# A decoder block with latent attention and gated linear attention: where its gate tiles are made, how v is spilled, and two smaller moves

## The chip, the cores and the metric

The kernel runs on one core of one Trainium2 chip. The metric is the device time of one execution in microseconds, from three runs. The core has TensorE (matmul; the profile calls it PE, and PEld its weight loads), VectorE (DVE), ScalarE (ACT), GpSimd (POOL) and SyncE (SP, which here only issues transfers).

## The reference, cut to what matters

With x of 1024 positions and 1024 channels, one layer computes

```
h = rmsnorm(x, g_in);  proj = h @ w_in
c_q, c_kv, k_r, z_mla, q_g, k_g, v_g, a_lr, z_gla, gate_mla, gate_gla = split(proj)
q = rmsnorm(c_q) @ w_uq  (8 heads, 64 + 32 columns, the 32 with rotary);  k_nope, v_mla = rmsnorm(c_kv) @ w_ukv
o_mla = softmax(q k^T / sqrt(96), causal) v_mla;  y_mla = (o_mla * silu(z_mla)) @ w_proj_mla
o_gla = chunked gated linear attention(q_g, k_g, v_g, log_a)  (4 heads, k 128, v 256)
y_gla = (rmsnorm(o_gla) * silu(z_gla)) @ w_proj_gla
out = rmsnorm(x + (sigmoid(gate_mla) * y_mla + sigmoid(gate_gla) * y_gla) @ w_out, g_final)
```

All in float32. The kernel keeps that precision by splitting each operand into a rounded part and a rest ("hi" and "lo", tiles named `...h` and `...l`) and adding three matmuls, hi x hi, hi x lo and lo x hi.

## The kernel before

The 1024 positions are two halves of 512. The program has these stages, in this order:

1. Projections of both halves together (`blocks`, matmuls at L390, tiles `prod`). VectorE and ScalarE add products (L732), split operands (`split`, L193 cast on ScalarE, L194 subtraction, on VectorE) and turn the results into what later stages read; these go to HBM: `gqd` (q, k and k transposed of the linear attention, split), `gvd` (its v, transposed, split), `latd`, `szd`, `xnd` (the normalised x of half 1).
2. Gated linear attention, 8 groups (2 halves x 4 heads). `fetch` loads a group's `qk` and `vv`; `scores_and_states`, `outputs`, `normalise` and `turn` work one group behind another. `tables` makes the rotary tables for each half beside it.
3. Attention of half 0 (8 heads), output of half 0 (`yg`, `ym` and `wo` units), then the same for half 1.

Beside stages 2 and 3 runs a stream of units (`Stream`): each has weights that are loaded (L161, tile `wraw`), split (L170 and L171, tiles `whi` and `wlo`; the subtraction goes to VectorE or GpSimd as the unit says) and used in steps of 6 matmuls (L184, tile `pj`). The units of a half stand in one list: gate tiles (`g0` to `g15`, 24 matmuls of 512 columns, tanh at L806 into `zr`, then stored to `gtd` from ScalarE's queue at L807), `uqr` (rotary part of the queries), `uv`, `hi0` to `hi3` (queries and keys of two heads each), `yg`, `ym`, `wo`. `GATES[h]` says how many gate tiles stand before `uqr` and after each `hi`: (10, 2, 2, 1, 1) for half 0 and (1, 4, 5, 4, 2) for half 1. The stream stops at a unit that is fenced, until the main program opens it. The main program calls `st.step(n)` between its own parts, so the gates are the work that TensorE does while a head waits for other engines. A list scheduler then sets the order of each engine.

One head of the attention: `row_max` computes scores against the keys a first time (L1240), adds the mask to the diagonal block (L1245), takes the maximum (L1247), and puts its negative into two extra query rows (L1255, L1256, L1261, L1264); this is done one head ahead. `scores` then computes the scores (L1284 to L1287), adds the mask (L1289), takes the exponential (L1293), splits it (L1296, L1297), sums it on GpSimd (L1299), and `values` multiplies by v (L1305, L1306). `linear_inputs` loads the linear attention's result during heads 5 and 6 in eight pieces of 256 KB through two `zr` buffers and splits each. The query tile `qt` holds 64 columns from `hi`, the 32 rotary ones (copied by ScalarE at L869 from `qr`) and the two extra rows.

In the output of half 0, `prologue` loads `xnd` in eight pieces and splits it into `xh` and `xl`, the operands of half 1's gates; those can start only afterwards (fence `1g0`).

## Time and profile before

| | us |
|---|---|
| median of three runs (1125.98 to 1134.52) | 1129.0 |
| the profiled execution | 1128.2 |
| its span, first to last instruction | 1126.4 |
| mean granted clock of TensorE | 0.962 |

The profile is of that one execution. A row by stage gives, for each engine, the time that it was busy in the stretch and the number of instructions; PEclk is the mean granted clock as a share of 2.4 GHz, and the last columns are the busy share of the 16 DMA engines and what they moved. A row of a group of instructions gives their line, engine, operation, out<-in with shapes and count, then busy time and mean ns of one, then the idle time of the engine just before them with what ended it. In a timeline a row is start, length, engine, line, operation, and in brackets the idle time before it and what ended that. "ACTq" is a transfer issued by ScalarE's queue, "SPq" one issued by SyncE's.

### The profile page before, as it was taken

How to read it: one execution, taken by the hardware profiler on the slowest of the kernel's cores; microseconds unless marked ns; L12 is line 12 of the kernel's file. 1: busy time of each engine (PE TensorE's matmuls, PEld its weight loads, DVE VectorE, ACT ScalarE, POOL GpSimd, SP SyncE). 2: the span in 40 equal slices, each digit the busy share in tenths (PEclk: the TensorE clock that was granted, in tenths of full speed). 3: DMA queues.
4: the chain of work that ended last, by engine and by line, in shares of the span. 5: the costliest groups of instructions: out<-in, count | busy, mean ns of one | idle time of the engine just before them, and what ended most of it. 6: DMA issues, size and time to landing. Idle time of an engine off the chain costs nothing.

```text
span 1126.4 us, 14090 instructions
## 1 busy us (share of the span) xinstructions
PE 1048.0 (93%) x4817; PEld 845.8 (75%) x4817; DVE 762.3 (68%) x1305; ACT 584.6 (52%) x1074; POOL 228.5 (20%) x173
## 2 busy tenths in 40 slices
PE   8999998999999878997898889999899999899997
PEld 4878887888888667875676667888678786678775
DVE  6885678788886535856766766476656768677463
ACT  5754374656574316765566553254565557434232
POOL 0000000000000000021433222123455555233320
PEclk9999999999999989999989779999999999899899
DMA  7452648555735598986624237744733233324432
GB/s 283 169 202 81 232 145 299 203 189 186 251 123 187 177 399 294 325 325 211 220 68 122 85 93 273 248 143 152 213 105 107 85 108 122 110 84 132 158 113 94
DMA packets 83992, 200.34 MB, mean 178 GB/s; under 512 B 8704, under 2 KB 21376, under 8 KB 83792
## 3 DMA queue, kind: packets, MB, share of 16 engines
q1 hardware_dynamic: 75856, 182.66, 48.1%
q10 hardware_dynamic: 8064, 16.78, 4.0%
q8 instruction: 38, 0.62, 0.2%
q14 instruction: 34, 0.28, 0.1%
HBM read 135.57 MB, written 63.83 MB: 177 GB/s over the span
## 4 chain that ended last, share of the span: by engine, by line
PE 37%; DVE 7%; ACT 3%; DMA 3%; issue 2%; POOL 1%; POOLq 0%; DVEq 0%; ACTq 0%; SPq 0%
PE pj L184 23%; PE y L924 2%; PE y L922 2%; PE y L923 2%; PE sc L1284 2%; DVE pl L1297 1%; DVE mx L1247 1%; PE sc L1286 1%; PE sc L1287 1%; PE ov L1306 1%; PE sc L1240 1%; PE ov L1305 1%; DMA zr<-gtd 1%; DMA wraw<-in_dram 1%; DMA kb<-krsp 1%
## 5 line engine op out<-in xcount | busy, mean ns | idle before, releaser
L184 PE MATMUL pj<-xl,whi 128*128 128x512 f32 x384 | 139.2, 411 | 2.1 <-ACT xl L193 2.1
L170 ACT CAST whi<-wraw 128x1024 fp32r<-128x1024 f32 (+2 forms) x84 | 85.0, 1012 | 94.4 <-PE pj L184 65.8
L184 PE MATMUL pj<-xh,whi 128*128 128x512 f32 x256 | 106.1, 414 | 17.1 <-ACT whi L170 14.7
L1299 POOL TENSOR_TENSOR acc<-acc,p 128x512 f32<-128x512 f32 (+3 forms) x80 | 85.4, 1068 | 151.3 <-ACT p L1293 137.5
L171 POOL TENSOR_TENSOR wlo<-wraw,whi 128x1024 fp32r<-128x1024 f32 (+2 forms) x33 | 73.6, 2230 | 94.7 <-ACT whi L170 54.3
L184 PEld LDWEIGHTS pj<-xl,whi 128*128 128x128 f32 x384 | 76.9, 201 | 18.7 <-ACT xl L193 2.5
L1297 DVE TENSOR_TENSOR pl<-p,ph 128x512 fp32r<-128x512 f32 (+3 forms) x80 | 69.7, 878 | 27.1 <-ACT ph L1296 27.0
L171 DVE TENSOR_TENSOR wlo<-wraw,whi 128x1024 fp32r<-128x1024 f32 x51 | 66.3, 1299 | 29.5 <-ACT whi L170 24.4
L732 DVE TENSOR_TENSOR ring<-prod,ring 128x512 f32<-128x512 f32 x85 | 58.4, 688 | 40.8 <-PE prod L390 38.0
L246 POOL TENSOR_TENSOR orn<-ms,mhalf 128x4 f32<-128x4 f32 x8 | 8.4, 1049 | 343.5 <-DMA zr<-in_dram 284.1
L184 PE MATMUL pj<-lat,whi 128*128 128x512 f32 x264 | 76.5, 429 | 0.1
L184 PEld LDWEIGHTS pj<-xh,whi 128*128 128x128 f32 x256 | 51.1, 200 | 28.6 <-ACT whi L170 15.5
L1293 ACT ACTIVATE p<-sc 128x512 f32<-128x512 f32 (+3 forms) x80 | 37.3, 469 | 65.7 <-DVE sc L1289 42.0
L184 PE MATMUL pj<-xh,wlo 128*128 128x512 f32 x256 | 70.3, 397 | 0.0
L193 ACT CAST w7h<-sw 128x512 fp32r<-128x512 f32 x68 | 41.8, 619 | 51.4 <-PE prod L390 45.9
L1247 DVE TENSOR_REDUCE mx<-sc 128x1 f32<-128x512 f32 (+2 forms) x96 | 51.7, 552 | 23.3 <-PE sc L1240 22.3
L184 PEld LDWEIGHTS pj<-lat,whi 128*128 128x128 f32 x264 | 53.5, 208 | 12.4 <-issue 0.6
L184 PEld LDWEIGHTS pj<-xh,wlo 128*128 128x128 f32 x256 | 48.1, 191 | 9.8
L390 PE MATMUL prod<-xl,w7h 128*128 128x512 f32 x136 | 54.1, 399 | 1.4 <-DVE xl L194 1.4
L390 PE MATMUL prod<-xh,w7h 128*128 128x512 f32 x136 | 54.7, 403 | 0.3 <-ACT w7h L193 0.2
L193 ACT CAST w7h<-raw 128x512 fp32r<-128x512 f32 x51 | 31.3, 619 | 38.2 <-PE prod L390 32.8
L924 PE MATMUL y<-whi,zl 128*128 128x512 f32 x128 | 50.4, 396 | 0.7 <-DVE zl L194 0.7
(300 smaller groups left out, 2706.7 us busy)
## 6 DMA issues: line engine op xcount, KB each, us to landing
wraw<-in_dram SPq DMA_DIRECT2D x74, 512.0 KB, 4.0
raw<-in_dram SPq DMA_DIRECT2D x32, 512.0 KB, 4.0
qk<-gqd SPq DMA_DIRECT2D x24, 512.0 KB, 6.5
gqd<-hl SPq DMA_DIRECT2D x16, 512.0 KB, 4.7
gvd<-hl SPq DMA_DIRECT2D x16, 512.0 KB, 3.6
vv<-gvd SPq DMA_DIRECT2D x16, 512.0 KB, 5.9
gtd<-zr ACTq DMA_DIRECT2D x32, 256.0 KB, 2.1
zr<-gtd SPq DMA_DIRECT2D x32, 256.0 KB, 2.9
```

Of the source, the lines that this page charges most:

```text
L170: nc.scalar.copy(out=hi[:, 0:n], in_=raw[:, 0:n])
L171: getattr(nc, lo_engine).tensor_tensor(out=lo[:, 0:n], in0=raw[:, 0:n], in1=R(hi[:, 0:n]), op=ALU.subtract)
L184: nc.tensor.matmul(out=ps, lhsT=a, rhs=b, start=(i == 0), stop=(i == 3 * n - 1))
L193: cast = nc.scalar.copy(out=hi, in_=src)
L390: mm = nc.tensor.matmul(out=ps, lhsT=a, rhs=b, start=(j == 0 and i in (1, 6, 7, 5)), stop=(j == 11), skip_group_check=True)
L732: nc.vector.tensor_tensor(out=t, in0=ps, in1=y, op=ALU.add)
L922: nc.tensor.matmul(out=c.ops[t], lhsT=a[0], rhs=b[0], start=(k == 0), stop=False)
L924: nc.tensor.matmul(out=c.ops[t], lhsT=a[1], rhs=b[0], start=False, stop=(k == 7))
L1247: nc.vector.reduce_max(mx[:, t, b:b + 1], ps[:, 0:n], axis=mybir.AxisListType.X)
L1293: nc.scalar.activation(p[:, 0:n], ps[:, 0:n], AF.Exp, scale=SCALE)
L1297: nc.vector.tensor_tensor(out=pl[:, 0:n], in0=p[:, 0:n], in1=R(ph[:, 0:n]), op=ALU.subtract)
L1299: nc.gpsimd.tensor_tensor(out=s.acc[:, q0:TH], in0=s.acc[:, q0:TH], in1=p[:, 0:n], op=ALU.add)
```

## The change

- Gates. `GATES` becomes (12, 4, 0, 0, 0) for half 0 and (0, 4, 3, 2, 1) for half 1, and the first six gate tiles of half 1 move into half 0's list: three before `hi2`, two before `hi3`, one before `yg0`. For these the rest of the weights (`wlo`) is made on VectorE. `gtd` gets a slot for each half.
- So that half 1's `xh` and `xl` exist by then, `prologue` runs during head 1 of half 0, through the two `zr` buffers; `m2` and `uh`, `ul` of half 0, which used the memory of `xh` and `xl`, get their own.
- Fewer steps of the stream in the heads of half 1 (5 in each of heads 0 to 5 and 12 in heads 6 and 7, where it was 11 in each); 6 in each head of half 0 instead of 4 and then 8.
- v is spilled in float32, unsplit: one store of 256 KB from ScalarE's queue for each piece instead of one of 512 KB from SyncE's, and `fetch` loads one 512 KB tile `vr` and splits it on chip instead of loading two.
- The second group's `fetch` stands behind three weight loads instead of beside the first. `gla` and `gla2` change places in memory, and `wgs`, `rst` and `gst` move.
- Mask and row maximum become one VectorE instruction for the block that has the diagonal (with a second one that reads the accumulator), and the maximum over both blocks of half 1 is chained through it.
- The rotary query rows `qt[64:96]` are moved by a transfer from SyncE's queue instead of a ScalarE copy.

```diff
-GATES = ((10, 2, 2, 1, 1), (1, 4, 5, 4, 2))
+GATES = ((12, 4, 0, 0, 0), (0, 4, 3, 2, 1))
+BORROW = (3, 2, 1)
...
-            rv = mk(pl, [P, TH], F32, "xs", bufs=bufs)
+            rv = mk(up, [P, TH], F32, "zr", bufs=2)
             nc.sync.dma_start(out=rv, in_=xnd[kt])
...
-                    o = hl()
-                    split(o[:, 0, :], o[:, 1, :], tp)
-                    move(gvd[h, g, vt], o)
+                    o = ring()
+                    nc.scalar.copy(out=o, in_=tp)
+                    nc.scalar.dma_start(out=gvd[h, g][:, vt, :], in_=o)
...
-                    nc.scalar.copy(out=qt[64:96], in_=R(c.qr[rr, hd // 4]))
+                    move(qt[64:96], c.qr[rr, hd // 4])
...
+    us0, us1 = units_of(0), units_of(1)
+    ahead = us1[:sum(BORROW)]
+    del us1[:sum(BORROW)]
+    for n, name in zip(BORROW, ("0hi2", "0hi3", "0yg0")):
+        k = next(i for i, u in enumerate(us0) if u.name == name)
+        us0[k:k] = ahead[:n]
+        del ahead[:n]
...
+            vr = mk(gp2, [P, 2, 4, P], F32, "vr")
+            nc.sync.dma_start(out=vr, in_=gvd[h, g].rearrange("p a (c f) -> p a c f", c=4))
             vv = mk(gp2, [P, 2, 2, 4, P], F32R, "vv")
-            for vt in range(2):
-                move(vv[:, vt].rearrange("p a c f -> p a (c f)"), gvd[h, g, vt])
+            split(vv[:, 0], vv[:, 1], vr)
...
         fetch(*cores[0])
-        fetch(*cores[1])
         for _ in range(4):
-            st.step(2)
+            st.step(3)
+        with tc.issue_after(loads[-3].ins):
+            fetch(*cores[1])
...
-                            nc.vector.tensor_tensor(out=ps[:, n - P:n], in0=ps[:, n - P:n], in1=msk[:, 1, :],
-                                                    op=ALU.add)
-                        nc.vector.reduce_max(mx[:, t, b:b + 1], ps[:, 0:n], axis=mybir.AxisListType.X)
+                            nc.vector.tensor_tensor_reduce(out=ps[:, 0:n], in0=ps[:, 0:n], in1=mrow[:, TH - n:TH], scale=1.0,
+                                                           scalar=NEG if b == 0 else mx[:, t, 0:1], op0=ALU.add,
+                                                           op1=ALU.max, accum_out=mx[:, t, b:b + 1])
+                        else:
+                            nc.vector.reduce_max(mx[:, t, b:b + 1], ps[:, 0:n], axis=mybir.AxisListType.X)
...
+                if hd == 1 and h == 0:
+                    lin = prologue()
...
-                    tick((1 if hd < 5 else 2) if h == 0 else (1, 2, 1, 1, 2, 1, 2, 1)[kt])
+                    tick((2, 1, 2, 1)[kt] if h == 0 else ((1, 0, 1, 1, 0, 1, 1, 0) if hd < 6 else (2, 1) * 4)[kt])
+                    if hd == 1 and h == 0:
+                        next(lin, None)
+                        if kt == 3:
+                            for _ in lin:
+                                pass
+                            st.fences.discard("1g0")
```

SyncE's queue where the linear attention begins, before: the weights of the third gate (the last row but two) stand behind both groups' `qk` (3822 to 3826 the first group's, 3831 to 3835 the second's) and the first `vv`.

```order
L161 DMA wraw<-in_dram 128x1024 x2
L991 DMA msk<-in_dram 128x384
L203 DMA qk_3822<-gqd 128x1024
L203 DMA qk_3824<-gqd 128x1024
L203 DMA szd<-ring 128x512
L203 DMA qk_3826<-gqd 128x1024
L203 DMA vv<-gvd 128x1024 x2
L203 DMA qk_3831<-gqd 128x1024
L203 DMA qk_3833<-gqd 128x1024
L203 DMA qk_3835<-gqd 128x1024
L161 DMA wraw<-in_dram 128x1024
L203 DMA vv<-gvd 128x1024 x2
```

The same place after, from the first group's v on (`vr`); 3914 and 3916 are the second group's `qk`, and L164 is the weight load.

```order
L1081 DMA vr<-gvd 128x1024
L1154 DMA sz<-szd 128x512 x2
L206 DMA lat_5284<-latd 128x1024
L164 DMA wraw<-in_dram 128x1024
L206 DMA lat_5284<-latd 128x1024 x2
L164 DMA wraw<-in_dram 128x1024
L206 DMA lat_5284<-latd 128x1024 x2
L1209 DMA um<-sncd 128x512
L1210 DMA um<-sncd 128x512
L164 DMA wraw<-in_dram 128x1024
L206 DMA qk_3914<-gqd 128x1024
L206 DMA qk_3916<-gqd 128x1024
```

Three weight loads and the five `lat` loads of the next stage now stand ahead of the second group's fetch.

TensorE in head 1 of half 0, from its first scores on, before; `pj<-xh,whi` and `pj<-xl,whi` are gate matmuls, `sc<-kb` the first scores of the next head's row maxima, `rs` the row sums of the head before.

```order
L1284 MATMUL sc<-qt,kb_5240 128x512
L1286 MATMUL sc<-qt,kb_5240 128x512
L1287 MATMUL sc<-qt,kb_5240 128x512
L1240 MATMUL sc<-kb_5241,qt 128x128
L1240 MATMUL sc<-kb_5241,qt 128x256
L184 MATMUL pj<-xh,whi 128x512
L184 MATMUL pj<-xl,whi 128x512
L184 MATMUL pj<-xh,whi 128x512
L184 MATMUL pj<-xl,whi 128x512
L184 MATMUL pj<-xh,whi 128x512
L184 MATMUL pj<-xl,whi 128x512
L1322 MATMUL rs<-ah,onh 128x512
```

The same place after.

```order
L1296 MATMUL sc<-qt,kb_5311 128x512
L1298 MATMUL sc<-qt,kb_5311 128x512
L1299 MATMUL sc<-qt,kb_5311 128x512
L1254 MATMUL sc<-kb_5312,qt 128x128
L1254 MATMUL sc<-kb_5312,qt 128x256
L1317 MATMUL ov<-ph,vm 128x128
L1334 MATMUL rs<-ah,onh 128x512
L1318 MATMUL ov<-pl,vm 128x128
L1296 MATMUL sc<-qt,kb_5311 128x384
L1298 MATMUL sc<-qt,kb_5311 128x384
L1299 MATMUL sc<-qt,kb_5311 128x384
L1254 MATMUL sc<-kb_5312,qt 128x384
```

In head 1 no gate matmul stands between the scores any more; the next ones come after its last scores.

ScalarE in head 1 of half 0, before: `acc` and `p` are the exponentials, `whi` and `zr` belong to the gates, `qt<-qr` is the copy of rotary rows.

```order
L1293 ACTIVATE acc<-sc 128x512
L1296 CAST ph<-acc 128x512
L1293 ACTIVATE p<-sc 128x384
L170 CAST whi<-wraw 128x1024
L1296 CAST ph<-p 128x384
L806 ACTIVATE zr<-pj 128x512
L807 DMA gtd<-zr 128x512
L1293 ACTIVATE p<-sc 128x256
L869 CAST qt<-qr 32x1024
```

The same place after; `xh<-zr` is the cast of a piece of half 1's x (L196 is `split`).

```order
L196 CAST xh<-zr 128x512
L1305 ACTIVATE acc<-sc 128x512
L1308 CAST ph<-acc 128x512
L196 CAST xh<-zr 128x512
L1305 ACTIVATE p<-sc 128x384
L1308 CAST ph<-p 128x384
L196 CAST xh<-zr 128x512
L1305 ACTIVATE p<-sc 128x256
L1308 CAST ph<-p 128x256
```

The casts of half 1's x stand between the exponentials where the gates' casts and the copy of rotary rows stood.

## Rows read from the trace of the kernel before

**Rows 1.** Page, part 1: busy time, share of the span, instructions of each engine.

```profile
PE 1048.0 (93%) x4817; PEld 845.8 (75%) x4817; DVE 762.3 (68%) x1305; ACT 584.6 (52%) x1074; POOL 228.5 (20%) x173
```

**Rows 2.** Busy time by stage: stretch, its length, engines, PEclk, DMA share, GB/s.

```profile
core 0: us, PE busy (x) PEld busy (x) DVE busy (x) ACT busy (x) POOL busy (x), PEclk, DMA share, GB/s
0.00:388.00 388.00, 378.72 (x1780) 306.83 (x1781) 293.76 (x499) 212.48 (x389) 6.27 (x10) 1.00 0.55 193
388.00:420.00 32.00, 21.46 (x97) 17.73 (x97) 9.66 (x17) 7.30 (x11) 0.00 (x0) 0.84 0.99 378
420.00:510.00 90.00, 81.58 (x480) 70.31 (x479) 59.68 (x123) 58.35 (x145) 12.38 (x9) 0.98 0.90 317
510.00:530.00 20.00, 13.47 (x88) 10.85 (x88) 13.69 (x32) 13.75 (x44) 2.01 (x2) 0.98 0.67 217
552.00:575.00 23.00, 18.74 (x78) 14.88 (x76) 12.48 (x29) 10.40 (x17) 8.23 (x5) 0.85 0.38 132
575.00:586.00 11.00, 10.23 (x52) 8.50 (x52) 7.80 (x23) 7.95 (x14) 4.29 (x4) 1.00 0.34 96
586.00:617.00 31.00, 26.38 (x123) 20.83 (x122) 21.27 (x47) 19.13 (x35) 10.35 (x10) 0.94 0.39 121
617.00:665.00 48.00, 39.59 (x147) 30.38 (x147) 33.04 (x76) 27.10 (x52) 10.56 (x12) 0.72 0.31 93
779.00:801.00 22.00, 19.72 (x84) 15.17 (x83) 18.51 (x26) 13.29 (x21) 12.61 (x7) 1.00 0.81 220
839.00:945.00 106.00, 102.58 (x471) 82.03 (x469) 73.92 (x126) 64.58 (x110) 61.51 (x42) 0.98 0.31 103
945.00:975.00 30.00, 24.89 (x102) 18.88 (x100) 26.05 (x45) 20.05 (x35) 7.89 (x7) 0.91 0.47 141
```

**Rows 3.** Timeline of 405 to 416 us, ScalarE, VectorE and TensorE.

```profile
412.43 0.33 ACTq L807 DMA_DIRECT2D gtd<-zr  x1
412.80 0.60 ACT L806 ACTIVATE zr<-pj 128x512 f32<-128x512 f32 x1 [11.89 <-DMA sz<-szd]
...
414.44 1.04 ACT L170 CAST whi<-wraw 128x1024 fp32r<-128x1024 f32 x1 [1.04 <-DMA lat<-latd]
...
415.51 1.23 DVE L171 TENSOR_TENSOR wlo<-wraw,whi 128x1024 fp32r<-128x1024 f32 x1 [7.23 <-ACT whi L170]
...
415.54 0.80 PE L184 MATMUL pj<-xh,whi 128*128 128x512 f32 x1 [5.77 <-ACT whi L170]
```

**Rows 4.** The chain that ended last, a stretch of matmuls without a wait.

```profile
681.88 10.53 PE pj L184 x46
```

**Rows 5.** Transfers by issue: queue, count, KB each, median us from issue to landing.

```profile
vv<-gvd SPq DMA_DIRECT2D x16, 512.0 KB, 5.9
...
kb<-krsp SPq DMA_DIRECT2D x6, 128.0 KB, 5.4
```

**Rows 6.** Groups of VectorE in 801 to 1048 us, shapes kept apart.

```profile
L1297 DVE TENSOR_TENSOR pl<-p,ph 128x512 fp32r<-128x512 f32 x32 | 40.7, 1276 | 6.5 <-ACT ph L1296 6.4
L1247 DVE TENSOR_REDUCE mx<-sc 128x1 f32<-128x512 f32 x40 | 27.4, 686 | 22.5 <-PE sc L1240 22.3
...
L1245 DVE TENSOR_TENSOR sc<-sc,msk 128x128 f32<-128x128 f32 x32 | 9.3, 291 | 4.1 <-PE sc L1240 3.8
...
L1297 DVE TENSOR_TENSOR pl<-acc,ph 128x512 fp32r<-128x512 f32 x8 | 5.5, 689 | 3.5 <-ACT ph L1296 3.5
```

**Rows 7.** Groups of VectorE in 0 to 388 us, shapes kept apart: the scan.

```profile
L585 DVE TENSOR_TENSOR_SCAN ab<-rst,mn 128x512 f32<-128x512 f32 x8 | 9.5, 1213 | 0.0
```

**Rows 8.** Groups of ScalarE in 801 to 1048 us: the copy of rotary rows.

```profile
L869 ACT CAST qt<-qr 32x1024 fp32r<-32x1024 f32 x6 | 6.3, 1045 | 0.3
```

**Rows 9.** Groups of GpSimd in 801 to 1048 us: a unit's low half.

```profile
L171 POOL TENSOR_TENSOR wlo<-wraw,whi 128x1024 fp32r<-128x1024 f32 x14 | 34.7, 2475 | 33.7 <-ACT whi L170 15.0 <-issue 6.8 <-PE pj L184 4.8
```

**Rows 10.** Timeline of ScalarE, 636 to 660 us (heads 5 and 6 of half 0).

```profile
649.72 0.62 ACT L193 CAST lat<-zr 128x512 fp32r<-128x512 f32 x1 [1.70 <-DMA zr<-ugd]
...
653.71 0.62 ACT L193 CAST qr<-zr 128x512 fp32r<-128x512 f32 x1 [0.93 <-DMA zr<-ugd]
```

More of the change, by code (lines that the diff above doesn't have):

```diff
@@ L156, in view @@
         return f.rearrange("p (a b c) -> p a b c", a=shape[0], b=shape[1])
+    loads = []
     def load_raw(spec):
@@ L160, in load_raw @@
         raw = mk(wrp, [P, 1024], F32, "wraw")
-        nc.sync.dma_start(out=view(raw, shape), in_=src)
+        loads.append(nc.sync.dma_start(out=view(raw, shape), in_=src))
         return raw
@@ L226, in hybrid_mla_gla_block_kernel @@
     sncd = dram.tile([2, 2, P, TH], F32, tag="sncd", name="sncd")
-    gtd = dram.tile([16, P, TH], F32, tag="gtd", name="gtd")
+    gtd = dram.tile([2, 16, P, TH], F32, tag="gtd", name="gtd")
     vsp = dram.tile([P, 4, HEADS, P], F32R, tag="vsp", name="vsp")
@@ L233, in hybrid_mla_gla_block_kernel @@
     gqd = dram.tile([2, 4, 3, P, 2, TH], F32R, tag="gqd", name="gqd")
-    gvd = dram.tile([2, 4, 2, P, 2, TH], F32R, tag="gvd", name="gvd")
+    gvd = dram.tile([2, 4, P, 2, TH], F32, tag="gvd", name="gvd")
     latd = dram.tile([2, 5, P, 2, TH], F32R, tag="latd", name="latd")
@@ L260, in hybrid_mla_gla_block_kernel, with prologue @@
     hv = [Half(), Half()]
-    def prologue(pl, bufs):
+    def prologue():
         c = hv[1]
@@ L558, in hl @@
                 return mk(hlp, [P, 2, TH], F32R, "hl")
-            consts(ring)
+            wgs = mk(skp, [P, 512], F32R, "wgs")
+            rst = mk(skp, [P, TH], F32, "rst")
+            consts(ring, wgs, rst)
             dk, lss, nlat = {}, {}, {}
@@ L806, in _ @@
                 nc.scalar.activation(zr, c.ps, AF.Tanh, scale=0.5)
-                nc.scalar.dma_start(out=gtd[i], in_=zr)
+                nc.scalar.dma_start(out=gtd[h, i], in_=zr)
         gates = iter(range(16))
-        for _ in range(GATES[h][0]):
+        for _ in range(GATES[h][0] or sum(BORROW)):
             gate_unit(next(gates), "vector")
@@ L887, in _ @@
                 t2 = mk(up, [P, TH], F32, "zr", bufs=2)
-                nc.sync.dma_start(out=t2, in_=gtd[8 + j])
+                nc.sync.dma_start(out=t2, in_=gtd[h, 8 + j])
                 if j == 0:
-                    c.m2 = mk(xgp, [P, 8, TH], F32, "xh")
+                    c.m2 = mk(c.lat2, [P, 8, TH], F32, "m2") if h == 0 else mk(xgp, [P, 8, TH], F32, "xh")
                 nc.vector.scalar_tensor_tensor(out=c.m2[:, j, :], in0=t2, scalar=onec, in1=ps, op0=ALU.add,
@@ L902, in _ @@
                     t2 = mk(up, [P, TH], F32, "zr", bufs=2)
-                    nc.sync.dma_start(out=t2, in_=gtd[j])
+                    nc.sync.dma_start(out=t2, in_=gtd[h, j])
                     nc.vector.scalar_tensor_tensor(out=t2, in0=t2, scalar=onec, in1=ps, op0=ALU.add, op1=ALU.mult)
@@ L961, in units_of, with consts @@
         return us
-    def consts(ring):
+    def consts(ring, wgs, rst):
         graw = ring()
@@ L989, in hybrid_mla_gla_block_kernel @@
     junk = mk(cs2, [P, 512], BF16, "junk")
-    gst = [mk(cs2, [P, 256], F32, f"gst{g}") for g in range(4)]
     nc.sync.dma_start(out=msk, in_=msk_d)
     def consts2():
+        nc.vector.memset(mrow, 0.0)
+        nc.vector.tensor_copy(out=mrow[:, TH - P:TH], in_=msk[:, 1, :])
         nc.vector.tensor_copy(out=idr, in_=idn)
@@ L1021, in hybrid_mla_gla_block_kernel @@
         gps = pool("glaps", 1, PSUM, stack=gs2)
+        gp2 = pool("gla2", 2, stack=gs2)
         gp = pool("gla", 1, stack=gs2)
-        gp2 = pool("gla2", 2, stack=gs2)
         gb = pool("glab", 1, stack=gs2)
         gb2 = pool("glab2", 2, stack=gs2)
+        gst = [mk(gb, [P, 256], F32, f"gst{g}") for g in range(4)]
         css = [slice(i * P, (i + 1) * P) for i in range(4)]
@@ L1081, in scores_and_states @@
             (s.qh, s.ql, kh, kl, kth, ktl), vv = inputs.pop((h, g))
-            s.v = [(vv[:, :, 0, i, :], vv[:, :, 1, i, :]) for i in range(4)]
+            s.v = [(vv[:, 0, :, i, :], vv[:, 1, :, i, :]) for i in range(4)]
             dec = decs[:, g, h, :]
@@ L1413, in hybrid_mla_gla_block_kernel @@
             st.fences.discard(f"{h}wo00")
-            for _ in range(8):
-                st.step(2)
-                next(pro, None)
-                st.step(2)
-            for _ in pro:
-                pass
+            st.step(32)
         hs.close()
```

16 lines of the change are left out of this document (4 added, 12 removed).

## The prediction

> **What bounds the kernel now.** I read the page's engine line first, then the busy time by stage, then the places where TensorE stood still, and last the prices of single instructions. TensorE is busy for 1048.0 of 1126.4 us [rows 1], so the time is TensorE's work plus what it loses. By stage the reader is to see two kinds of loss [rows 2]: the stretch that is not busy, and the clock, where the granted clock (column PEclk) is below 1.00, that is where part of the stretch ran at 1.2 instead of 2.4 GHz. I add both: lost = length - busy + length x (1 - PEclk). That gives 9.3 us in 0:388 (projections); 15.7, 10.2 and 6.9 in 388:420, 420:510 and 510:530 (linear attention); 7.7, 0.8 and 6.5 in 552:575, 575:586 and 586:617 (heads 0 to 3 of half 0); 21.9 in 617:665 (heads 4 to 6); 2.3 in 779:801 (passage to half 1); 5.5 and 7.8 in 839:945 and 945:975 (heads 1 to 4, and 5, of half 1). So the loss is in the linear attention and in the heads of half 0, and the heads of half 1 are nearly full of TensorE work.
>
> The change removes no matmul (4784 in both orders). It moves gate tiles: one is 24 matmuls, and 46 such in a row take 10.53 us [rows 4], 0.229 each, so 5.5 us a tile. Counted in the two orders of TensorE, gate matmuls change by +48 in the linear attention, +96 before the end of head 3 of half 0 (96 to 192), -24 in the passage to half 1, -96 in heads 1 to 4 of half 1 (216 to 120) and -24 in its head 5 (48 to 24). The sum is 0; what decides is how much of the loss the moved tiles fill, and how much new loss they leave behind.
>
> **The change part by part.**
>
> Linear attention, 388:530. Matmuls: +48 x 0.229 = +11.0 us. Transfers: the three stretches move 32 x 378 + 90 x 317 + 20 x 217 = 44.9 MB at a DMA share of 0.99, 0.90 and 0.67 [rows 2]. One 512 KB `vv` load fewer for each of 8 groups [rows 5] is -4.2 MB; the rotary tables, whose loads and stores (by their shapes four of 256 KB, two more of 256, two of 128 and two of 64) the order now puts into the projections, -1.9; two gates' weights and results (0.5 + 0.25 MB each) +1.5. That is -4.6 MB, 12 to 15 us of transfers at 317 to 378 GB/s. The first stretch has the clearest stall: ScalarE issues `gtd<-zr` at 412.43 and starts its next instruction after 11.89 us without one, the third gate's cast follows at 414.44, and TensorE's matmul waits for that cast until 415.54 [rows 3]. Before it, SyncE had queued both groups' fetches; now the second fetch (2 instead of 2.5 MB) stands behind three weight loads. I take 7 of the 15.7 us back here. In the two later stretches 17.1 us are lost, and the 11 us of added gates fall into them, the last 24 matmuls near the end, where before no gate stood; I take 12 back. Sum: 11 - 19 = -8. Bounds: nothing comes back, +11; all but 5 of the 32.8 comes back, -17. Splitting v on chip costs a cast (1.04 us for 128x1024 [rows 3]) and a subtraction (1.23) in each group; ScalarE was busy 58 and VectorE 60 of 90 us [rows 2], and the 28 table instructions leave VectorE here. That cover holds unless the split is last before a group's outputs.
>
> Projections, 0:388. 16 subtractions of v leave VectorE and the 28 table instructions arrive, between the 76th and the 82nd of its 89 additions to a product. TensorE loses only 9.3 of 388 us there [rows 2], and its operands are prepared three products ahead. I take +1; bounds -2 and +10 (half of 28 x 0.69, if TensorE has to wait for its operands).
>
> Half 0 up to head 3, 552:617. +96 x 0.229 = +22.0 us. The order puts 30 gate matmuls around the wait for head 0's maxima, where 7.7 us were lost; I take 6 back. Head 1 now has no gate until its last scores, and eight casts of `xh` stand in ScalarE's order in heads 0 and 1. The nearest rows are heads 5 and 6, where eight casts wait for their loads in the same way (`lat` 1.70 us, then `qr` 0.93 [rows 10]) and 617:665 loses 0.45 us in each. Head 1 with 16 us instead of 11 then loses 8. Heads 2 and 3 are full and give back 4.5. `qt<-qr`, 1.05 us of ScalarE a head [rows 8], becomes a transfer that the order issues as soon as its buffer is free; the nearest row, a 128 KB load into 32 partitions, lands in 5.4 us [rows 5], so a head gains 1.05 us where ScalarE is late and loses up to 4.4 where the row maxima wait for it and SyncE has weight loads queued behind. I take -0.5 for heads 0 to 3 together. Sum 22.0 - 6 + 8 - 4.5 - 0.5 = +19; bounds +12 and +27.
>
> Heads 4 to 6, 617:665. The same gates as before; three ScalarE copies (3.1 us) leave. The fused maximum replaces a mask addition (291 ns) and a reduction (686 at 512 columns) [rows 6] by one instruction and a read of the accumulator. No row shows it. From below it costs what the reduction alone does (saves 0.29); from above what a 512-column scan of two operands does, 1213 ns [rows 7] (costs 0.24). I take -0.2, nearer the plain additions and reductions, all 0.69: -0.8 us a head on VectorE, half of it on the path. Sum -2; bounds -5 and +3.
>
> Passage to half 1, 779:801. One gate fewer, -5.5 us, but the chain after the last output (rotation, copies, first loads) does not shorten with it, so most of the 5.5 becomes idle: -2; bounds -5.5 and +2. The eight casts that leave the output stage lay beside matmuls that never stopped there: 0.
>
> Heads 1 to 4 of half 1, 839:945. -96 x 0.229 = -22.0 us leaves 84 of 106. VectorE was busy for 73.9 [rows 2]; without four masks and with the fused maxima it needs about 70, 83% of 84. Heads with little TensorE work took longer than their VectorE time: 617:665 has 33.0 in 48 (69%), 945:975 has 26.1 in 30 (87%). At 78% the four heads take 90 us: -16. Bounds: 84 (-22), and 101 at 69% (-5).
>
> One rule speaks to this term. `pl` of 512 columns takes 1276 ns on average here and 689 as `pl<-acc` at the start of a head, when GpSimd adds nothing [rows 6]; a gate's low half on GpSimd takes 2475 [rows 9], and four of them leave these heads. The Trainium skill (SBUF — State Buffer, Who interferes with whom) says that a VectorE instruction with two SBUF inputs and a GpSimd one that reads SBUF exclude each other for a whole instruction. The two means agree with that; by it, four low halves fewer would free VectorE at the latest for 4 x 2.5 = 10 us, and the heads could fall to their TensorE time.
>
> Head 5, 945:975: -5.5 of matmuls, but VectorE has 26.05 of the 30 us and loses about 1: 28, -2; bounds -5 and 0. The rest is unchanged.
>
> Sum: -8 + 1 + 19 - 2 - 2 - 16 - 2 = -10. The profiled execution took 1128.2 us, so 1118; the median of the runs, 1129.0, is 0.8 higher, and I keep 1118.
>
> **The rivals.**
>
> A. Heads that are thin in gates fall to half clock. For it: 617:665 has a granted clock of 0.72 though TensorE is busy for 82% of it; 839:945 has 0.98 with its gates. If heads 1 to 4 of half 1 ran at 0.80, their 80 us of work would take 20 us more than at full clock, some 16 more than I allow: 1134, slower than before. Against it: 575:586 kept 1.00. It ends above the time of before from a clock of about 0.86 down. The Trainium skill (TensorE: Matmul & The Clock Gate, HAM oscillation) says that a loop whose matmuls come in bursts with waits between is set back again and again; rows 2 agree in 617:665.
>
> B. The linear attention gives nothing back for its two gates, because its chain from group to group decides and not its transfers: +4 instead of -8, 1130. For it: in 420:510 TensorE is already busy for 81.6 of 90. Against: the DMA share.
>
> C. It is the transfers: all of the 12 to 15 us and the stall go, -17: 1109.
>
> D. GpSimd's share: the heads of half 1 fall to 84 us: 1118 - 6 = 1112.
>
> E. The change does not do what it says: the query rows, moved to spare ScalarE, arrive late. At 4.4 us for four of the eight pairs of heads that is 17: 1135. SyncE's order issues them ahead of need, so I give it little.
>
> **How the numbers follow.** My sum 0.35 (1112 to 1124), A 0.17, B 0.18, C 0.17, D 0.08, E 0.05. About 1% is what a measurement of this kernel can tell from no change (three runs span 0.8%). Below 1117.7: C, D and 0.45 of my sum's 0.35, with a little of B, 0.43. Above 1140.3: half of A, a third of B and E with the upper bounds, 0.15. Between: 0.42. The range 1098 to 1139 leaves out what lies beyond C with a good head 1, and A and E together. The likeliest case's own range is 1112 to 1124.
>
> **What would show it.** Right: the stall at 412 gone and 388:530 some 8 us shorter; 552:617 longer by about 19 with head 1 its emptiest part; heads 1 to 4 of half 1 at some 22.5 us each, VectorE near 78%, clock above 0.9; the fused maximum near 0.7 us at 512 columns. Wrong: a linear attention as long as before or longer, a halved clock in the heads of half 1, row maxima waiting for the `qt` transfer, or head 1 no emptier than the others.

## The result, and the profile after

The changed kernel takes 1135.2 us (median of 14 runs, 1128.4 to 1140.7) against 1127.0 for the kernel before (14 runs, 1123.9 to 1134.5): a ratio of 1.0067, 95% interval 1.0044 to 1.0090. It is slower by 0.7%, where I forecast 1118, faster by 1%.

The profiled execution of the changed kernel took 1128.4 us and is the shortest of the 14, so its stages, which add up to the same span as before, understate what a usual run takes by some 7 us; where those 7 us lie was not profiled. They still tell how the time moved between the stages. Page, part 1, after:

```profile
PE 1045.0 (93%) x4817; PEld 845.6 (75%) x4817; DVE 758.5 (67%) x1298; ACT 571.7 (51%) x1064; POOL 213.5 (19%) x166
```

The totals answer to [rows 1] and tell nothing: every engine is as busy as before or a little less. The stages do. Busy time by stage, after, with the columns of [rows 2]; I cut at the end of the last product, at the first scores for row maxima, and at the first `mt` matmul of a head:

```profile
0.00:418.80 418.80, 389.15 (x1781) 314.04 (x1781) 301.94 (x513) 219.78 (x397) 6.27 (x10) 0.96 0.50 174
418.80:576.00 157.20, 143.08 (x794) 122.87 (x794) 97.23 (x174) 90.50 (x215) 22.34 (x14) 0.96 0.80 286
576.00:654.40 78.40, 73.38 (x343) 60.66 (x343) 46.59 (x109) 43.45 (x78) 19.43 (x17) 0.96 0.52 162
600.50:615.40 14.90, 11.26 (x46) 8.86 (x45) 14.30 (x32) 11.40 (x24) 3.75 (x4) 0.77 0.59 184
654.40:694.10 39.70, 33.96 (x144) 26.40 (x142) 31.93 (x77) 26.27 (x51) 11.99 (x11) 0.83 0.47 137
694.10:848.20 154.10, 148.12 (x629) 118.22 (x627) 90.69 (x122) 54.34 (x84) 42.04 (x29) 0.97 0.59 179
869.20:953.80 84.60, 79.94 (x367) 62.15 (x366) 66.12 (x122) 52.86 (x97) 49.57 (x37) 1.00 0.35 103
953.80:977.90 24.10, 19.70 (x80) 14.41 (x79) 23.40 (x42) 17.27 (x33) 7.72 (x7) 0.86 0.51 147
```

The kernel before, cut at the same events (its projections end at 388.4):

```profile
0.00:388.40 388.40, 379.12 (x1781) 306.85 (x1781) 293.76 (x499) 212.48 (x389) 6.27 (x10) 1.00 0.55 193
388.40:552.30 163.90, 136.93 (x746) 115.25 (x746) 99.68 (x192) 92.12 (x216) 20.95 (x14) 0.95 0.84 300
552.30:616.90 64.60, 54.99 (x247) 43.88 (x245) 41.55 (x96) 37.40 (x64) 22.88 (x18) 0.92 0.38 120
616.90:664.60 47.70, 39.26 (x141) 30.08 (x142) 33.04 (x76) 27.18 (x53) 10.56 (x12) 0.71 0.31 94
839.30:944.70 105.40, 101.98 (x464) 81.60 (x463) 73.32 (x125) 63.98 (x109) 61.19 (x42) 0.98 0.32 104
944.70:975.40 30.70, 25.56 (x106) 19.46 (x105) 26.40 (x45) 20.35 (x36) 7.91 (x8) 0.90 0.47 138
```

| stage | before | after | difference | forecast |
|---|---|---|---|---|
| projections | 388.4 | 418.8 | +30.4 | +1 |
| linear attention, up to the first row maxima | 163.9 | 157.2 | -6.7 | -8 |
| heads 0 to 3 of half 0 | 64.6 | 78.4 | +13.8 | +19 |
| heads 4 to 6 | 47.7 | 39.7 | -8.0 | -2 |
| from there to head 0 of half 1 | 153.3 | 154.1 | +0.8 | -2 |
| heads 1 to 4 of half 1 | 105.4 | 84.6 | -20.8 | -16 |
| head 5 | 30.7 | 24.1 | -6.6 | -2 |
| head 6 | 31.7 | 29.2 | -2.5 | 0 |

All but the first line came out within 3 us of the forecast or better. The projections alone, for which I had forecast 1 us and at most 10, took 30 more. For the same 1781 matmuls TensorE was busy 10.0 us longer (389.15 against 379.12, at a mean granted clock of 0.96 instead of 1.00) and idle 20.4 us longer (29.7 against 9.3). The waits of TensorE up to 420 us, after (who waited for whom, total, times, longest):

```profile
PE prod L391 <- ACT w7h L196: 14.3, 3, 6.1
PE prod L391 <- DVE ring L735: 4.7, 2, 4.5
PE prod L391 <- ACT ring L747: 4.5, 1, 4.5
```

They are, above all, four stops: 6.1 us at 224, 4.5 at 283, 5.6 at 346 (the first three sit at the same point of three decays) and 4.5 at 407. Busy time around the third of them:

```profile
340.00:360.00 20.00, 14.39 (x53) 11.34 (x52) 14.81 (x28) 11.41 (x29) 0.00 (x0) 0.83 0.36 129
```

The stops add up to 20.7 us, as much as the idle time that came in. The longer busy time goes with the clock: in the stretch of the third stop it is 0.83 on average, that is, part of it ran at 1.2 GHz. Together they are the 30 us. ScalarE around the first stop, after (start, length, engine, line, operation; in brackets the idle time before):

```profile
220.02 1.16 ACT L665 ACTIVATE ring<-ring 128x512 f32<-128x512 f32 x2
...
221.59 0.61 ACT L196 CAST w7h<-sw 128x512 fp32r<-128x512 f32 x1
224.52 0.69 ACT L611 ACTIVATE ep<-ab,sb 128x128 f32<-128x128 f32 x2 [2.32 <-DVE ns L604]
...
228.91 0.39 ACT L612 ACTIVATE mn<-ab,ns 128x128 f32<-128x128 f32 x1
229.20 0.61 ACT L665 ACTIVATE ring<-ring 128x512 f32<-128x512 f32 x1
...
229.82 0.60 ACT L196 CAST w7h<-sw 128x512 fp32r<-128x512 f32 x1
230.33 0.62 ACT L665 ACTIVATE ring<-ring 128x512 f32<-128x512 f32 x1
230.86 0.56 ACT L747 COPY ring<-prod 128x512 f32<-128x512 f32 x1
```

ScalarE runs the 16 exponentials of a decay in one piece, 224.5 to 229.2, and the cast of the next weight (`w7h`, 229.82), for which TensorE has waited since 224.4, stands behind them, with three writers of `ring` beside it. ScalarE was not short of time: it sat idle for 2.3 us just before. It is the order that differs. In the kernel before, at the same point, the copy of a product (L744) and the next weight's cast stand ahead of the exponentials (L608):

```profile
222.74 0.57 ACT L744 COPY ring<-prod 128x512 f32<-128x512 f32 x1
...
225.51 0.62 ACT L193 CAST w7h<-sw 128x512 fp32r<-128x512 f32 x1 [1.16 <-PE prod L390]
229.19 0.69 ACT L608 ACTIVATE ep<-ab,sb 128x128 f32<-128x128 f32 x2 [3.05 <-DVE ns L601]
```

### The profile page after: what moved, and what is told of

Same layout as the page of the kernel before. It is cut to its first block, busy times and chain, and to the rows that moved or that the text cites. A ratio compares the mean times of both kernels' runs of the same rounds, so it can differ in the third digit from the quotient of the medians.

```text
span 1126.3 us, 14118 instructions
## 1 busy us (share of the span) xinstructions
PE 1045.0 (93%) x4817; PEld 845.6 (75%) x4817; DVE 758.5 (67%) x1298; ACT 571.7 (51%) x1064; POOL 213.5 (19%) x166
## 4 chain that ended last, share of the span: by engine, by line
PE 36%; DVE 6%; DMA 3%; ACT 2%; issue 2%; POOL 1%; SPq 0%; POOLq 0%; DVEq 0%; ACTq 0%
PE pj L187 22%; PE y L927 2%; PE y L926 2%; PE y L925 2%; PE sc L1296 2%; PE sc L1298 1%; PE sc L1299 1%; PE sc L1254 1%; PE ov L1317 1%; PE ov L1318 1%; DMA zr<-gtd 1%; DVE mx L1263 1%; DVE wlo L174 1%; DVE sc L1259 1%; DMA zr<-ugd 1%
## 5 line engine op out<-in xcount | busy, mean ns | idle before, releaser
L1311 POOL TENSOR_TENSOR acc<-acc,p 128x512 f32<-128x512 f32 (+3 forms) x80 | 88.1, 1101 | 150.6 <-ACT p L1305 137.0
L187 PE MATMUL pj<-xl,whi 128*128 128x512 f32 x256 | 103.4, 404 | 0.0
L174 DVE TENSOR_TENSOR wlo<-wraw,whi 128x1024 fp32r<-128x1024 f32 x58 | 76.2, 1315 | 27.2 <-ACT whi L173 23.1
L196 ACT CAST w7h<-sw 128x512 fp32r<-128x512 f32 x68 | 42.1, 620 | 81.8 <-PE prod L391 78.2
L1309 DVE TENSOR_TENSOR pl<-p,ph 128x512 fp32r<-128x512 f32 (+3 forms) x80 | 66.2, 835 | 18.1 <-ACT ph L1308 17.5
L174 POOL TENSOR_TENSOR wlo<-wraw,whi 128x1024 fp32r<-128x1024 f32 (+2 forms) x26 | 55.8, 2149 | 118.5 <-ACT whi L173 51.6
L187 PE MATMUL pj<-lat,whi 128*128 128x512 f32 x264 | 72.7, 404 | 0.0
L197 DVE TENSOR_TENSOR w7l<-sw,w7h 128x512 fp32r<-128x512 f32 x68 | 46.6, 686 | 30.8 <-PE prod L391 26.1
L391 PE MATMUL prod<-xh,w7h 128*128 128x512 f32 x136 | 57.0, 420 | 10.3 <-ACT w7h L196 5.6
L187 PEld LDWEIGHTS pj<-lat,whi 128*128 128x128 f32 x264 | 50.0, 194 | 10.4 <-issue 0.4
L187 PEld LDWEIGHTS pj<-xl,whi 128*128 128x128 f32 x256 | 50.0, 195 | 9.8
L196 ACT CAST w7h<-raw 128x512 fp32r<-128x512 f32 x51 | 31.2, 618 | 39.3 <-PE prod L391 31.7
```

What stands on the lines that cost most here:

```text
L174: getattr(nc, lo_engine).tensor_tensor(out=lo[:, 0:n], in0=raw[:, 0:n], in1=R(hi[:, 0:n]), op=ALU.subtract)
L187: nc.tensor.matmul(out=ps, lhsT=a, rhs=b, start=(i == 0), stop=(i == 3 * n - 1))
L196: cast = nc.scalar.copy(out=hi, in_=src)
L197: rest = (lo_engine or nc.vector).tensor_tensor(out=lo, in0=src, in1=R(hi), op=ALU.subtract)
L391: mm = nc.tensor.matmul(out=ps, lhsT=a, rhs=b, start=(j == 0 and i in (1, 6, 7, 5)), stop=(j == 11), skip_group_check=True)
L1309: nc.vector.tensor_tensor(out=pl[:, 0:n], in0=p[:, 0:n], in1=R(ph[:, 0:n]), op=ALU.subtract)
```

## The experiments

All times are medians, all ratios against the kernel before on the same chip; the kernel before took 1127.6 to 1128.9 us in these sets. A run and the base that it is compared with can come from two chips, between which the kernel before differs by up to 1.3 us; differences of a few us between runs of four executions are rough.

### What broke the projections

Three parts of the change touch the projections: v's float32 copy takes buffers of `ring` instead of `hl` (two pools of buffers that the results of the projections pass through; `ring` has nine, of 2 KB in each partition, which both ScalarE and VectorE write), its store goes out from ScalarE's queue, and the rotary tables come in. First v as before, all else changed:

```diff
-                    o = ring()
-                    nc.scalar.copy(out=o, in_=tp)
-                    nc.scalar.dma_start(out=gvd[h, g][:, vt, :], in_=o)
+                    o = hl()
+                    split(o[:, 0, :], o[:, 1, :], tp)
+                    move(gvd[h, g, vt], o)
```

> The changed kernel with v split and spilled as before (hl tile, 512 KB from SyncE's queue, two loads per group); all else as changed. Seen so far: in the changed kernel the projections end at 418.8 us instead of 388.4, with TensorE standing still for 6.1, 4.5, 5.6 and 4.5 us at 224, 283, 346 and 407 us and 12 us more lost to a granted clock of 0.83 to 0.93 around them. Theory R (ring): v's float32 copies take buffers of `ring`, so that ScalarE's other writers of `ring` come later in its order, behind the 16 exponentials of a decay, with a weight cast behind them. Then the first three stalls go (16.2 us and about 10 of clock), the projections end near 392, and with 4 MB of transfers back in the linear attention the time is about 1113 (1105 to 1120). Theory T (tables): it is the 28 rotary-table instructions in the projections. Then the stalls stay and the time is 1135 to 1142.

Measured: 1115.2 us, ratio 0.988 (0.986 to 0.991). The projections end at 389.5, the stops of 4 us and more are gone, as R says. But without the tile `vr` the tables moved too: the second of the two starts only at 421.8 us, in the linear attention. So this run alone does not part R from T.

Then the spill kept, but its buffer changed:

```diff
-                    o = ring()
+                    o = R(hl()[:, 0, :])
```

> The changed kernel with v's float32 copy written into half of an `hl` tile instead of a `ring` tile; the store from ScalarE's queue, the single load and the split on chip stay. R: two or three of the stalls at 224, 283 and 346 go, the time is 1108 to 1119. T: no change, 1135. A third theory S (the stores issued from ScalarE's queue, 0.33 us each, delay its casts): no change either, 1135, with the weight casts still behind the exponentials.

Measured: 1110.8 us, 0.985 (0.981 to 0.988); the projections end at 397.6. Theory S falls, since the stores are still there. The tables are all in the projections, where their first operation stands in the view of tile `ang` (count, ns min/median/max, first and last start):

```profile
L1049 DVE CAST ang<-pi x2: 426/428/429, 351.8 to 368.5; 128x512 f32<-128x512 int32 x2
```

The first three stops are gone all the same, so T falls as their cause too. ScalarE at the first of the three places in this run:

```profile
220.12 0.63 ACT L665 ACTIVATE ring<-ring 128x512 f32<-128x512 f32 x1
...
221.16 0.62 ACT L196 CAST w7h<-sw 128x512 fp32r<-128x512 f32 x1
223.28 0.63 ACT L665 ACTIVATE ring<-ring 128x512 f32<-128x512 f32 x1 [1.50 <-DVE ring L735]
223.82 0.57 ACT L747 COPY ring<-prod 128x512 f32<-128x512 f32 x1
225.29 0.71 ACT L611 ACTIVATE ep<-ab,sb 128x128 f32<-128x128 f32 x2 [0.90 <-DVE ns L604]
...
229.72 0.39 ACT L612 ACTIVATE mn<-ab,ns 128x128 f32<-128x128 f32 x1
230.01 0.61 ACT L196 CAST w7h<-sw 128x512 fp32r<-128x512 f32 x1
```

The activation and the copy that write `ring` now stand ahead of the exponentials, and TensorE stops for 1.1 us instead of 6.1. The cast of the next weight still stands behind the exponentials; that it is the copy at L747, which empties a product's tile, that keeps TensorE going is read from the order and was not tested by itself.

The spill alone in the kernel before (the lines on v in the diff under The change, nothing else):

> The kernel before with the v spill alone changed (float32 in a `ring` tile, store from ScalarE's queue, one load, split on chip). R: the three stalls appear in it, some 27 us more in the projections, less 4 to 8 for the transfers spared in the linear attention: about 1148 (1140 to 1155). T: no stalls, faster by the transfers alone, about 1121.

Measured: 1148.0 us, 1.019 (1.015 to 1.023), the value that R gave. Its projections end at 415.0, with waits of 14.7 us for `w7h` and 4.5 for L747, and its tables all stand in the linear attention:

```profile
L1036 DVE CAST ang<-pi x2: 414/414/414, 444.9 to 478.6; 128x512 f32<-128x512 int32 x2
```

Stops without the tables here, tables without the stops in the run before: the first three stops come with v's buffer. The linear attention falls from 163.9 to 158.5.

Is it the sharing of the ring, or is the ring too short by one? The same 2 KB, once as a buffer of v's own and once as a tenth buffer of the ring (each an edit of the changed kernel):

```diff
+            vrp = pool("vring", 1, stack=s1)
...
-                    o = ring()
+                    o = mk(vrp, [P, TH], F32, "vcp")
```

> The changed kernel with v's float32 copy in a buffer of its own (a pool of one tile, 2 KB). Sharing decides: the three stalls go and the projections end at 390 to 396, 1105 to 1111. The number of buffers decides: one is not enough, 1125 to 1135.

```diff
-            rgp = pool("ring", 9, stack=s1)
+            rgp = pool("ring", 10, stack=s1)
```

> The changed kernel with ten `ring` buffers instead of nine, v still in the ring: the same 2 KB. Sharing decides: stalls as in the changed kernel, 1135. Number: 1105 to 1115.

Measured: 1113.2 us (ratio 0.986, 0.979 to 0.992) with a buffer of v's own, projections 393.5; 1135.5 (1.005, 1.002 to 1.008) with the tenth buffer, projections 417.6. TensorE's waits there with ten buffers:

```profile
PE prod L391 <- ACT w7h L196: 11.2, 2, 5.6
PE prod L391 <- ACT ring L747: 7.0, 2, 4.5
```

One more buffer in the ring changes nothing; the same buffer kept for v alone removes the stops, so for them it is the sharing. The time, 1113.2, is above the 1105 to 1111 that I had set for it: the linear attention of that run takes 163.5 us instead of the 156.0 of the run with v in an `hl` tile. Why was not found.

The tables: `gla` and `gla2` in their old order, with v in an `hl` tile.

> As the run with v in half of an `hl` tile, and the pools `gla` and `gla2` in their old order, which puts the 28 rotary-table instructions back into the linear attention. R and T each in part: the stall at 407 goes too, worth 4.5 us and 1.8 of clock, less what 28 VectorE instructions cost in the linear attention: 1102 to 1112. If the place of the tables is indifferent: as the run with v in an `hl` tile, within 3 us.

Measured: 1112.2 us, 0.985 (0.983 to 0.988). The projections shorten from 397.6 to 391.0, the linear attention grows from 156.0 to 160.2 (VectorE 96.5 to 112.5 us busy there), and 2.7 us are lost between the halves. The place of the tables costs 6.6 us in the projections and gives about as much back elsewhere. The fourth stop, near the end of the projections, has two parents: it is 4.5 us in the changed kernel, 3.6 with v in an `hl` tile, 2.0 with a buffer of v's own, 3.0 with v in the ring but no tables, and absent here.

### The parts of the change, one by one

From here the base is the run with v in an `hl` tile. ScalarE's copy of the query rows back:

```diff
-                    move(qt[64:96], c.qr[rr, hd // 4])
+                    nc.scalar.copy(out=qt[64:96], in_=R(c.qr[rr, hd // 4]))
```

> From here on the run with v in half of an `hl` tile (1110.8 us) is the base. This one is the base with the rotary query rows copied by ScalarE again, in all 16 heads. Theory Q (the transfer spares ScalarE 1.05 us in a head where it is on the path): slower than the base by 3 to 8 us. Theory L (rival E of the prediction: the transfers come late): in the base the first row maxima of half 1 stand still for 5.0 us and then run at half clock, while the three `qt` transfers issued there take 10.6 us to land; then this run is faster than the base by 3 to 8 us, all of it between the output of half 0 and head 1 of half 1.

Measured: 1105.3 us, 0.980 (0.976 to 0.985), 5.5 us faster than the base (whose interval, 0.981 to 0.988, overlaps this one). The stages and the wait show theory L, in one place: from head 7 of half 0 to head 0 of half 1 the base takes 156.5 us and this run 150.2. The base's wait of TensorE there:

```profile
PE sc L1254 <- DMA qt<-qr: 5.0, 1, 5.0
```

Here that wait is absent. Head 1 of half 0, where ScalarE also casts half 1's x, is 2.9 us longer with the copies, so both theories hold, in different heads. Copies in heads 0 to 2 of half 1 alone, with the tables in the linear attention:

> The run with v in an `hl` tile and the tables in the linear attention (1112.2 us), with the query rows of heads 0 to 2 of half 1 alone copied by ScalarE. There the first row maxima of half 1 stood still for 7.4 us. Theory L (they wait for the `qt` transfers, 12.6 us from issue to landing): that goes, 7 us and 3 of clock: 1102 to 1106. If they wait for another of the loads that are queued there (`vo`, `ko`, `wraw`): 1110 to 1113.

Measured: 1101.4 us, 0.979 (0.975 to 0.982), clear of the 0.983 to 0.988 of its base; the stretch between the halves takes 148.9 us instead of 159.2, and of this set it has the lowest median.

Mask and maximum apart again:

> The base with mask and row maximum as two VectorE instructions again. In the changed kernel's rows the fused one takes 757 ns at 512 columns and the read of its accumulator 137, against 291 and 686 before: 83 to 94 ns saved in each, and the maximum over two blocks (151 ns) in each head of half 1, so some 0.4 to 0.5 us of VectorE a head, 7 us in all. Theory V (VectorE is on the path in the heads): slower than the base by 3 to 7 us. Theory N (those heads wait for something else): the same within 2 us.

Measured: 1122.1 us, 0.995 (0.993 to 0.997): 11 us slower than the base, beyond both theories. Heads 4 to 6 of half 0 take 46.2 us instead of 39.9 and the stretch from there to the end of head 0 of half 1 6.3 us more; heads 1 to 4 of half 1 take as long as in the base. And the fused instruction alone in the kernel before:

> The kernel before with mask and row maximum fused, alone (for the room of `mrow`, `wgs` and `rst` move into the projections' memory). If the 11 us are the instruction's own: 1117 to 1121, heads 4 to 6 of half 0 at 41 instead of 48 us. If they belong to the order that the moved gates give the heads: 1123 to 1127.

Measured: 1120.3 us, 0.993 (0.990 to 0.996); heads 4 to 6 of half 0 take 41.6 us instead of 47.7, head 5 of half 1 27.8 instead of 30.7. So the gain, 8.6 us, comes without the moved gates. It is a net value: the linear attention of this run takes 4.0 us more than before (167.9), for which I have no reason. Prices of VectorE in 836 to 1037 us, after:

```profile
L1259 DVE CUSTOM_DVE_ANT_0 sc<-sc,mrow,mx 128x512 f32<-128x512 f32 x8 | 6.1, 757 | 0.7
...
L1259 DVE DVE_READ_ACCUMULATOR2_ANT mx<- 128x1 f32 x32 | 4.4, 137 | 0.0
```

757 + 137 against 291 + 686 [rows 6]: 83 ns saved, less than the 200 I took. Four such in a head are 0.3 us, yet heads 4 to 6 gain 2 us each. VectorE in head 4 shows one reason, first before:

```profile
628.31 0.30 DVE L1245 TENSOR_TENSOR sc<-sc,msk 128x128 f32<-128x128 f32 x1 [0.78 <-PE sc L1240]
628.52 1.21 DVE L171 TENSOR_TENSOR wlo<-wraw,whi 128x1024 fp32r<-128x1024 f32 x1
629.65 0.69 DVE L1247 TENSOR_REDUCE mx<-sc 128x1 f32<-128x512 f32 x1
```

and in the run with the fused instruction alone:

```profile
631.73 0.70 DVE L1248 CUSTOM_DVE_ANT_0 sc<-sc,mrow 128x512 f32<-128x512 f32 x1 [0.56 <-PE sc L1243]
632.35 0.14 DVE L1248 DVE_READ_ACCUMULATOR2_ANT mx<- 128x1 f32 x1
632.35 1.22 DVE L171 TENSOR_TENSOR wlo<-wraw,whi 128x1024 fp32r<-128x1024 f32 x1
```

Before, the order put a gate's low half between the mask and the maximum, and the head's maximum came 1.2 us later. One instruction leaves no gap to put anything in. That this accounts for all of the 6 us was not shown.

The second group's fetch right behind the first:

```diff
         fetch(*cores[0])
+        fetch(*cores[1])
         for _ in range(4):
             st.step(3)
-        with tc.issue_after(loads[-3].ins):
-            fetch(*cores[1])
```

> The base (v in half of an `hl` tile, 1110.8 us) with the second group's fetch issued right behind the first one's, as before. Theory F (the prediction's: the second fetch queued ahead of the third weight load makes ScalarE and TensorE stand still, 7 us): 1115 to 1119, with a stop of TensorE of some 5 us before a gate about 20 us into the linear attention. If the smaller v and the place of the tables gave that back by themselves: within 2 us of the base.

Measured: 1118.7 us, 0.993 (0.991 to 0.995), 7.9 us slower than the base, all of it in the linear attention (163.8 us against 156.0). TensorE waits for a gate's cast three times there (9.4 us in all) instead of once (4.8). The single stop of 5 us that I had expected came as two of 2.3.

### The gates

The base with the gates, their borrowing, half 1's x and the steps of the stream as before:

> The base with the gates as before: GATES of before, nothing borrowed, the load of half 1's x in the output of half 0, the steps of the stream in the heads as before. Theory G (the moved gates bring most of what the heads gained): 1124 to 1131, that is slower than the base by 13 to 20 us, with heads 1 to 4 of half 1 at 105 us instead of 84.5 and heads 0 to 3 of half 0 at 64 instead of 78. Theory Z (moving matmuls is a zero sum, and what was gained comes from the transfers, the maxima and the query rows): within 4 us of the base.

Measured: 1104.4 us, 0.979 (0.977 to 0.981): neither theory, it is 6.5 us faster than the base. The edit undoes the gates, the early load of half 1's x and the steps together. Busy time by stage in this run: heads 0 to 3 and 4 to 6 of half 0, heads 1 to 4 of half 1.

```profile
544.70:604.60 59.90, 53.99 (x247) 43.64 (x246) 35.77 (x96) 33.76 (x62) 23.30 (x19) 0.91 0.42 136
604.60:644.90 40.30, 33.34 (x143) 25.84 (x144) 31.40 (x77) 25.49 (x49) 10.75 (x12) 0.83 0.40 120
821.90:923.00 101.10, 99.65 (x464) 80.55 (x463) 70.60 (x122) 58.89 (x105) 62.69 (x42) 1.00 0.37 114
```

Against the base the moved gates cost 7.1 us in the linear attention (156.0 - 148.9), 19.0 in heads 0 to 3 (78.9 - 59.9) and give 16.6 back in heads 1 to 4 of half 1 (101.1 - 84.5).

Head 1 of half 0 is the emptiest of these heads (14.9 us, 11.3 busy, clock 0.77 in the changed kernel). Two of half 0's last gates kept for it:

```diff
-GATES = ((12, 4, 0, 0, 0), (0, 4, 3, 2, 1))
+GATES = ((12, 2, 2, 0, 0), (0, 4, 3, 2, 1))
```

> The run with tables in the linear attention and ScalarE copies in heads 0 to 2 of half 1 (1101.4 us), with two of half 0's last four gate tiles put behind `hi1` (GATES for half 0: 12, 2, 2, 0, 0). Head 1 of half 0 then has 36 gate matmuls instead of 12 before it ends. Theory H (head 1 loses 9 us and clock because no gate is left for it while half 1's x is loaded): faster by 4 to 8 us, 1093 to 1097. Rival: the eight loads and splits of half 1's x hold head 1 by themselves, and the gates only add to it: the same, within 2 us, or slower.

Measured: 1106.5 us, 0.981 (0.978 to 0.984), 5 us slower than its base. Its heads 0 and 1:

```profile
563.00:578.40 15.40, 14.52 (x54) 11.90 (x55) 8.64 (x23) 7.81 (x15) 2.36 (x3) 0.68 0.38 129
578.40:591.70 13.30, 13.04 (x67) 10.87 (x66) 8.82 (x23) 7.41 (x15) 2.23 (x3) 1.00 0.33 98
```

Head 1 is filled, 13.3 us at full clock instead of 16.9, but heads 0 to 3 together go from 79.5 to 83.1: head 0, from which the gates were taken, is now as long with 54 matmuls, at a granted clock of 0.68, as it was with 78 at full clock (15.4 and 15.6 us). In front of it, where TensorE waits for the first row maxima, 30 matmuls stand instead of 42, and TensorE is now idle for 3.2 of 9.5 us: the gates were filling that wait, and without them the loss moves from head 1 to head 0. Head 3 takes up the gates that are left (33.3 instead of 21.4 us). H was right of head 1 and wrong of the sum. The intervals of the two runs overlap: that the sum is no better is shown, that it is worse rests on the stages of one execution each.

With the gates as before the other remedies bring nothing more. The three runs:

> The run with the gates as before (1104.4 us), with the tables in the linear attention and ScalarE copies of the query rows in heads 0 to 2 of half 1. If both remedies add up as on the moved gates (6 us less in the projections and 4 more in the linear attention, 5 to 7 less between the halves): 1095 to 1099. If the gates of before already covered the late query rows: 1100 to 1104.

> As the run before it in this set, but with the tables left in the projections: tells which of the two remedies acts. Query rows late without the borrowed gates too: 1098 to 1101. Covered by the gates of before: 1104.

> All of the change but the gates, with v in a buffer of its own: 1104.4 us with v in an `hl` tile, where the projections ended at 395.8. They end at 390 to 392 by the sharing theory: 1098 to 1101. If the remaining 7 us there are due to the tables: 1104.

Measured: 1105.3, 1104.9 and 1107.3 us, against 1104.4. The gates of before cover the late query rows. With v in its own buffer the projections end at 395.7 as with an `hl` tile (with the moved gates it was 393.5 against 397.6), so most of the 7 us that remain there against before are not v's buffer; the two runs that put the tables back (391.0, and 390.6 with the gates as before) put them down to the tables. That the third run is 3 us above its 1104 lies in the linear attention, 156.4 us instead of 148.9, as in the other run with this buffer.

With ScalarE's copies of the query rows in, the moved gates are no slower than the gates as before: 1105.3 against 1104.9, and 1101.4 against 1105.3 with the tables moved too (all intervals overlap). So by these runs the 6.5 us that they cost in the base go with the late query rows, not with the gates alone.

The best versions take 1101 to 1105 us, some 2.1% less than the kernel before: v in an `hl` tile, and either the gates as before, or the moved gates with the tables in the linear attention and ScalarE's copies of the query rows in three heads. Their intervals overlap.

## Why the prediction was wrong, point by point

- **Projections, the step that failed.** The forecast was a gain of 10 us, the result a loss of 8. "16 subtractions of v leave VectorE and the 28 table instructions arrive ... I take +1; bounds -2 and +10": I counted VectorE's instructions and the tables, and left out which buffer the new copy takes and where ScalarE's order then puts the others that write it. Measured +30. v's buffer brings most of it: changing the buffer alone takes 21.2 us from the projections (418.8 to 397.6) and 24.3 from the whole time (1135.2 to 1110.8), and the spill alone in the kernel before adds 26.6 (388.4 to 415.0). The tables add 6.6 us, inside the bounds. With that one buffer elsewhere the changed kernel takes 1110.8, a little below the likeliest case's own range.
- **Linear attention, right in sum, in part by luck.** -6.7 for -8. The stop for the third gate's cast is gone (one of 4.8 us before the first gate stays, as before), and the fetch behind the weight loads is worth 7.9 us where I took 7. Of the 11 us of added gates only 4 were hidden (the gates alone cost 7.1), not most of them. What paid instead is the smaller v, worth 5.4 us alone in the kernel before (163.9 to 158.5), and the tables that left (4.2 by the run that put them back).
- **Heads 0 to 3 of half 0, right.** +13.8 for +19, inside the bounds. The 22.0 us of matmuls filled 8.2 us of loss where I took 3. Head 1 is the emptiest, as foretold (14.9 us, 11.3 of them busy).
- **Heads 4 to 6 and head 5 of half 1, mis-sized.** -8.0 and -6.6 for -2 and -2. In heads 4 to 6 the term is the fused maximum, -0.8 us a head with half of it on the path: the instruction saves less (83 ns), the heads gain more (6.1 us when it is alone), at least in part by what the order can no longer put in between. Head 5 is not its doing alone: from 30.7 us it falls to 27.8 with the fused maximum alone, and in the base it takes some 25 us with the mask and maximum apart, with the gates as before, and with neither undone.
- **Heads 1 to 4 of half 1, right in direction, not in what limits them.** -20.8 for -16, of which the gates bring 16.6. I had VectorE limit them, with 70 us of work at 78%. That its share came out at 78% is luck: its work was 66.1 us, and TensorE was busy for 79.9 of 84.6 us, so the heads fell nearly to TensorE's time. The fused maximum alone (105.1) and v alone (105.4) shorten these heads by nothing; where the other 4 us come from is open.
- **Rival A (half clock in thin heads)** fell: the granted clock of those heads is 1.00. (By its own sum it passes the time of before at a clock of about 0.84, not 0.86.) **Rival B** (the linear attention gives nothing back) fell. **Rival C** fell: 6.7 us with the gates in it, not 17.
- **Rival D** ended at its 84 us for the heads, but the low halves are not what brought them there. `pl` of 512 columns in heads 1 to 4 of half 1: in the kernel before, with nine low halves on GpSimd; in the changed kernel, with four (by these rows five leave, where I had counted four); and in the run with the gates as before, with nine:

```profile
L1297 DVE TENSOR_TENSOR pl<-p,ph 128x512 fp32r<-128x512 f32 x16 | 23.6, 1477 | 4.2 <-ACT ph L1296 4.2
```

```profile
L1309 DVE TENSOR_TENSOR pl<-p,ph 128x512 fp32r<-128x512 f32 x16 | 19.9, 1247 | 0.5 <-ACT ph L1308 0.5
```

```profile
L1302 DVE TENSOR_TENSOR pl<-p,ph 128x512 fp32r<-128x512 f32 x16 | 19.4, 1218 | 6.0 <-ACT ph L1301 6.0
```

  `pl` became 230 ns cheaper with the change, as D says, but putting the five low halves back does not make it dearer again. The rule of the Trainium skill (SBUF — State Buffer, Who interferes with whom) is not contradicted by this, since GpSimd's additions run beside `pl` in all three; what lowered the price is open.
- **Rival E (late query rows)** is real, at one place, between the halves: 5.0 us of waiting in the base, 5.5 us by the time. In the profile of the changed kernel itself TensorE waits 2.1 us there, so this is not what failed the forecast. I gave it 0.05 and thought of pairs of heads, where nothing waited.
- The range (1098 to 1139) held the time, by luck: its upper part stood for A and E, and neither is what happened. None of the rivals had the projections in it.
